# A hybrid linear-attention layer: the last set of 64x64 inverses taken up piece by piece inside the scan

## The chip, the cores and the metric

One core of a Trainium2 chip runs the whole layer in one launch. The metric is the device time of a run in microseconds (us); of several runs the median counts. The core's engines are TensorE (PE; its weight loads are listed as PEld), VectorE (DVE), ScalarE (ACT), GpSimd (POOL) and SyncE (SP), which here issues most DMA transfers. Each engine executes its instructions strictly in its own order; semaphores make them wait for one another.

## The reference

One layer: an adaLN-modulated RMSNorm, one input projection, and two token mixers side by side (a bidirectional chunked gated DeltaNet with 4 heads of 128, and windowed attention), then gates, projections and a residual. Sequence 2048 + 256 context tokens, width 1024. The part that the change concerns is the DeltaNet's chunk algebra (chunks of 64 tokens, two directions):

```python
a_mat = where(strict, einsum('nbhik,nbhjk->nbhij', kb, kc) * decay, 0)      # 64x64 per chunk and head
t_mat = triangular_solve(a_mat, eye, left_side=True, lower=True, unit_diagonal=True)
u = einsum('nbhij,nbhjv->nbhiv', t_mat, vc * bc)
w = einsum('nbhij,nbhjk->nbhik', t_mat, kb * exp(gc))
def step(s, xs):                              # sequential over the chunks
    v_new = u_n - einsum('bhck,bhkv->bhcv', w_n, s)
    s_new = s * exp(gl_n) + einsum('bhck,bhkv->bhkv', kd_n, v_new)
    o = einsum('bhck,bhkv->bhcv', qd_n, s) + einsum('bhij,bhjv->bhiv', qk_n, v_new)
```

Each `t_mat` is the inverse of a unit lower triangular 64x64 matrix. It depends on k, beta and the decays alone, not on the state, so all inverses can be had ahead of the scan.

## The kernel before, in words

The kernel runs in stages: norm and transposes, the state projection, q/k/v with their convolution, the products per chunk, then inverses, scan, attention, projections and output. The inverses are computed in three sets by forward substitution on DVE, 32 to 128 matrices side by side, one per partition. Two sets are made in `base`, beside matmuls of the gate projections. The last set is made by `base4`: it holds the 64-token blocks of the latent chunks 14 and 15 for the forward direction and 0 and 1 for the backward one (`LAST`), which the scan reaches only in its last two steps. It has 32 matrices, and each is handled as four groups of columns (column mod 4), so that it fills 128 partitions:

- two loads bring the raw blocks to `N` (L777, from `Nsp`), two more the betas;
- two DVE instructions scale `N` by columns and rows (L779, L780), each over all 64x64 of 32 partitions;
- three DMA copies take `N` to the other partitions (L784);
- 63 substitution rows of two DVE instructions each (L789 product into `btmp`, L791 sum into X, which is a slice of `btmp`);
- sixteen stores take X to DRAM (L796, `X4sp`).

The scan has 18 steps, each with both directions; step 0 and 1 are the context. A step of `chain` is, per direction: ksps = k·S on PE (L1085), x on DVE (L1087), vps on PE (L1091), v on DVE (L1094), sps on PE (L1103) and the state S on DVE (L1109); x begins as a load of v (L1077) with a multiplication on POOL (L1078). `merge` (L975 on) prepares the next step's 128x128 inverse from the 64x64 ones: it loads them (L995) or, for `LAST`, loads four parts into the single buffer `x4` (L990) and interleaves them on POOL (L991), then transposes (mtp: L1004, L1006), multiplies (myp, L1014 and L1016, scaled on DVE by L1018; mep, L1021 and L1023). `output` computes aps (L1126) and ops (L1137), with DVE's L1131, L1134 and L1138; partial outputs go to `osp` and come back when the other direction reaches the chunk.

Beside the scan run gate projections: `rps` matmuls (L524 to L526), 24 to a group, with their weight splits (L246 on DVE, L245 on POOL) and an `rt` step on DVE (L812). They do not depend on the scan and fill PE.

What sets the order: a scheduler takes instructions by priority with a model of the engines' timeline, and writes one fixed order for each engine. The scan is emitted at a higher priority than the gates around it. `base4` is emitted ahead of the scan, so its instructions are ahead of the scan's in priority; where they stand is what the scheduler makes of their readiness.

```python
    base4(*LAST)
    ...
        gates(list(range(4)), (1, 0))
        with tc.high_priority(tc.cur_priority):
            scan(scp, scl, cs)
        gates(list(range(4, BESIDE)), (1, 0))
```

The functions that the change touches, with their line numbers:

## Time and profile before

| | us |
|---|---|
| runs | 2027.2, 2026.38, 2021.74; median 2026.38 |
| profiled execution | 2024.6, span of its instructions 2022.9 |
| PE busy | 1943.7 (96%) |
| DVE busy | 1413.3 (70%) |
| ACT, POOL busy | 786.9 (39%), 656.8 (32%) |
| mean granted clock of TensorE | 0.986 of full |

The busy times are sums over the whole span; what an engine waits for is seen in the view of waits (for each line: what it waited for, total, times, longest) and in the timeline, where brackets hold the idle time ahead of an instruction and what ended it. The windows give each engine's busy time in a stretch and the granted clock there. The scan with its gates lies between 925 and 1375 us of the span.

### The profile page before, as it was taken

What the parts mean: (1) busy time and instruction counts of PE and PEld (TensorE: products, weight loads), DVE (VectorE), ACT (ScalarE), POOL (GpSimd) and SP (SyncE); (2) the same over time, 40 slices, a digit from 0 to 9 for tenths busy, and PEclk for the clock granted to TensorE, in tenths of its full rate; (3) what the DMA queues carried; (4) which work ended last, traced back from release to release, by engine and by line L of the source; (5) the groups of instructions that cost most, each with busy time, mean ns of one, the idle gap of its engine ahead of it and who ended that gap; (6) DMA issues with size and microseconds to landing.
All of it is one profiled execution on the core that took longest, in us unless ns stands there. A gap on an engine that the chain in (4) does not pass through costs nothing. (4 is left out here: it accounts for less than half of the span.)

```text
span 2022.9 us, 32038 instructions
## 1 busy us (share of the span) xinstructions
PE 1943.7 (96%) x11043; PEld 1630.9 (81%) x11043; DVE 1413.3 (70%) x2774; ACT 786.9 (39%) x1975; POOL 656.8 (32%) x751
## 2 busy tenths in 40 slices
PE   6999999989999899999999999999989999999999
PEld 3888888779898778787788888878777888878887
DVE  7979766667776999999699556635676878743322
ACT  6755545554343322111122223325665656531100
POOL 1742210224542211004222234323555443442221
PEclk8999999999999999999999999999999999999999
DMA  7552326755447633528877777664455555365542
GB/s 259 168 138 85 95 88 159 198 151 163 143 144 190 164 115 109 144 86 234 206 222 213 219 230 218 196 190 156 146 167 173 183 161 169 113 190 181 181 146 94
DMA packets 375511, 333.11 MB, mean 165 GB/s; under 512 B 83833, under 2 KB 299185, under 8 KB 374709
## 3 DMA queue, kind: packets, MB, share of 16 engines
q1 hardware_dynamic: 347924, 288.59, 49.4%
q10 hardware_dynamic: 27424, 42.48, 5.9%
q8 instruction: 87, 1.43, 0.3%
q14 instruction: 76, 0.61, 0.1%
HBM read 220.28 MB, written 109.13 MB: 163 GB/s over the span
## 5 line engine op out<-in xcount | busy, mean ns | idle before, releaser
L524 PE MATMUL rps<-hh,wh 128*128 128x512 f32 x768 | 308.4, 402 | 6.4 <-DVE rt L812 5.1
L526 PE MATMUL rps<-hh,wl 128*128 128x512 f32 x768 | 308.6, 402 | 0.0
L525 PE MATMUL rps<-hl,wh 128*128 128x512 f32 x768 | 308.5, 402 | 0.0
L524 PEld LDWEIGHTS rps<-hh,wh 128*128 128x128 f32 x768 | 145.4, 189 | 41.8 <-DVE rt L812 5.5
L563 DVE SCALAR_TENSOR_TENSOR cacc<-y,cw,cacc 128x512 f32<-128x512 f32 (+1 forms) x224 | 162.3, 746 | 22.7 <-ACT cacc L561 18.6
L524 PE MATMUL lps<-hh,wh 128*128 128x512 f32 (+1 forms) x448 | 171.5, 383 | 0.3 <-ACT y L634 0.3
L525 PEld LDWEIGHTS rps<-hl,wh 128*128 128x128 f32 x768 | 145.4, 189 | 32.4
L526 PE MATMUL lps<-hh,wl 128*128 128x512 f32 (+1 forms) x448 | 171.4, 382 | 0.0
L526 PEld LDWEIGHTS rps<-hh,wl 128*128 128x128 f32 x768 | 145.4, 189 | 32.0
L525 PE MATMUL lps<-hl,wh 128*128 128x512 f32 (+1 forms) x448 | 171.2, 382 | 0.0
L938 DVE TENSOR_TENSOR pl<-pt,ph 128x512 fp32r<-128x512 f32 x156 | 105.4, 685 | 43.7 <-ACT ph L936 42.9
L936 ACT CAST ph<-pt 128x512 fp32r<-128x512 f32 x156 | 90.4, 585 | 112.2 <-PE pt L934 77.8
L910 DVE CUSTOM_DVE_ANT_0 pr<-sc,band,sk 128x640 f32<-128x640 f32 (+1 forms) x128 | 106.5, 862 | 33.8 <-PE sc L906 18.1
L810 ACT ACTIVATE rt<-rps 128x512 f32<-128x512 f32 x96 | 57.3, 597 | 176.2 <-PE rps L526 162.6
L749 DVE TENSOR_TENSOR N<-N,btmp 128x62 f32<-128x62 f32 (+30 forms) x124 | 116.8, 942 | 3.0
L920 POOL TENSOR_SCALAR pr<-pr,sm 128x640 f32<-128x640 f32 (+1 forms) x128 | 99.7, 800 | 56.5 <-DVE sm L918 40.9
L747 DVE TENSOR_TENSOR btmp<-N 128x62 f32<-128x62 f32 (+30 forms) x124 | 114.8, 926 | 3.1
L912 ACT ACTIVATE pr<-pr,sm 128x640 f32<-128x640 f32 (+1 forms) x128 | 104.0, 815 | 19.6 <-DVE sm L910 19.6
L1216 PE MATMUL pps<-yh,wph 128*128 128x512 f32 x256 | 105.2, 415 | 5.8 <-ACT yh L1198 4.3
L246 DVE TENSOR_TENSOR wl<-wr,wh 128x512 fp32r<-128x512 f32 x120 | 92.6, 787 | 24.6 <-POOL wh L245 22.3
L245 POOL TENSOR_SCALAR wh<-wr 128x512 fp32r<-128x512 f32 x72 | 47.7, 678 | 180.1 <-PE lps L525 97.1
L1217 PE MATMUL pps<-yl,wph 128*128 128x512 f32 x256 | 101.5, 397 | 0.0
(301 smaller groups left out, 4944.9 us busy)
## 6 DMA issues: line engine op xcount, KB each, us to landing
wr<-in_w_in_dram SPq DMA_DIRECT2D x120, 256.0 KB
kw<-Ksp SPq DMA_DIRECT2D x28, 384.0 KB
x<-vsp SPq DMA_DIRECT2D x36, 256.0 KB
k<-ksp SPq DMA_DIRECT2D x34, 256.0 KB
kT<-kTsp SPq DMA_DIRECT2D x34, 256.0 KB
wm<-in_w_mod_dram SPq DMA_DIRECT2D x16, 512.0 KB
xt<-in_x_dram SPq DMA_DIRECT2D x16, 512.0 KB
dtl<-Dsp SPq DMA_DIRECT2D x32, 256.0 KB
```

Source lines behind the costliest of these rows:

```text
L524: T.matmul(ps, lhsT=wh[:, k], rhs=xh[:, k], start=k == 0, stop=False)
L525: T.matmul(ps, lhsT=wh[:, k], rhs=xl[:, k], start=False, stop=False)
L526: T.matmul(ps, lhsT=wl[:, k], rhs=xh[:, k], start=False, stop=k == kt - 1)
L563: V.scalar_tensor_tensor(a, y[:, t:t + n], cw[:, m, t:t + 1], a, op0=ALU.mult, op1=ALU.add)
L747: V.tensor_tensor(tv, A[:, m + 1:, m].unsqueeze(2).to_broadcast([h1 + n, r, m]), A[:, m, 0:m].unsqueeze(1).to_broadcast([h1 + n, r, m]), o ...
L749: V.tensor_tensor(A[:, m + 1:, 0:m], A[:, m + 1:, 0:m], tv, op=ALU.add)
L910: V.tensor_tensor_reduce(s_, ps[:, o:768], band[:, b0:b0 + W + 256], -0.125, sk[:, 1, hd:hd + 1], ALU.add, ALU.min, sm[:, h, 1:2])
L912: S.activation(s_, s_, AF.Exp, scale=-1.0, bias=sm[:, h, 1:2], accum_out=sm[:, h, 2:3])
L920: G.tensor_scalar(p[:, h, :W + 256], p[:, h, :W + 256], sm[:, h, 3:4], 1.0, op0=ALU.mult, op1=ALU.mult)
L938: V.tensor_tensor(pl, pt, f32(ph), op=ALU.subtract)
L1216: T.matmul(ps, lhsT=wh[:, k, ms], rhs=hs[k], start=k == 0, stop=False)
L1217: T.matmul(ps, lhsT=wh[:, k, ms], rhs=ls[k], start=False, stop=False)
```

## The change

`base4` becomes a generator that is taken up in pieces. The first piece (loads and the memsets on POOL) stays ahead of the scan. The second (scaling and the three copies) is taken at the end of scan step 2, then six substitution rows at the end of each of steps 3 to 12, the last three rows and the sixteen stores at step 13. Each piece is emitted back at the priority that holds outside the scan's block (`high_priority(-after)`), and not ahead of that step's last state update on the engine concerned (`issue_after`). The scaling is cut in four groups of 16 rows, each over its columns up to the diagonal's block: 16, 32, 48 and 64.

```diff
-        sh = [32, 64, 64]
-        V.tensor_tensor(N[0:32], N[0:32], nc_.unsqueeze(1).to_broadcast(sh), op=ALU.mult)
-        V.tensor_tensor(N[0:32], N[0:32], nb[0:32].unsqueeze(2).to_broadcast(sh), op=ALU.mult)
         G.memset(X, 0.0)
         for q in range(4):
-            if q:
-                dma(N[q * 32:q * 32 + 32], N[0:32])
             G.memset(X[q * 32:q * 32 + 32].rearrange("p r s -> p (r s)")[:, 16 * q:16 * q + 976:65], 1.0)
+        yield
+        for q in range(4):
+            r, w = slice(q * 16, q * 16 + 16), q * 16 + 16
+            V.tensor_tensor(N[0:32, r, 0:w], N[0:32, r, 0:w], nc_[:, 0:w].unsqueeze(1).to_broadcast([32, 16, w]), op=ALU.mult)
+            V.tensor_tensor(N[0:32, r, 0:w], N[0:32, r, 0:w], nb[0:32, r].unsqueeze(2).to_broadcast([32, 16, w]), op=ALU.mult)
+        for q in range(1, 4):
+            dma(N[q * 32:q * 32 + 32], N[0:32])
+        yield
         for m in range(63):
...
             V.tensor_tensor(X[:, m + 1:, 0:n], X[:, m + 1:, 0:n], tv, op=ALU.add)
+            if m % 6 == 5:
+                yield
...
                     dma(X4sp[d, ci, q], X[p0:p0 + 8])
+        yield
...
-    base4(*LAST)
+    last_base = base4(*LAST)
+    next(last_base)
...
+                last_S[0] = i
...
+            if 2 <= st < NC - 2:
+                with tc.high_priority(-after), tc.issue_after(last_S[0].ins):
+                    next(last_base, None)
...
-        with tc.high_priority(tc.cur_priority):
-            scan(scp, scl, cs)
+        first = tc.cur_priority
+        with tc.high_priority(first):
+            scan(scp, scl, cs, first)
```

In the changed kernel the lines of the scan are 6 to 9 further down: S is L1117, x L1095, rt L818, moff's scaling L1025, L1138 is L1147, the scaling L784 and L785, the copies L787, the substitution L792 and L794, the stores L801, the reads of `X4sp` L997.

The orders differ from here up to the end of the scan alone. First place, DVE around scan step 2. `N` is scaled, `my` and `moff` belong to the merge, `S` is the state, `oa` an output; the piece runs from the merge's L1012 (L1019) to the first output after the scaling. Before:

```order
L1012 TENSOR_TENSOR my_10504<-mtp,br 64x256
L779 TENSOR_TENSOR N<-N,btmp 32x4096
L246 TENSOR_TENSOR wl<-wr,wh 128x512
L812 SCALAR_TENSOR_TENSOR rt<-rt,rps 128x512
L246 TENSOR_TENSOR wl<-wr,wh 128x512
L1109 SCALAR_TENSOR_TENSOR S_10439<-S_10318,tot,sps 128x128 x4
L1109 SCALAR_TENSOR_TENSOR S_10477<-S_10351,tot,sps 128x128 x4
L1018 TENSOR_TENSOR moff_10486<-myp,br 64x256
L780 TENSOR_TENSOR N<-N,nb 32x4096
L1138 TENSOR_TENSOR oa_10542<-ops,oa_10542 128x512
```

Now:

```order
L1019 TENSOR_TENSOR my_10357<-mtp,br 64x256
L246 TENSOR_TENSOR wl<-wr,wh 128x512
L818 SCALAR_TENSOR_TENSOR rt<-rt,rps 128x512
L246 TENSOR_TENSOR wl<-wr,wh 128x512
L1117 SCALAR_TENSOR_TENSOR S_10292<-S_10171,tot,sps 128x128 x4
L1117 SCALAR_TENSOR_TENSOR S_10330<-S_10204,tot,sps 128x128 x4
L784 TENSOR_TENSOR N<-N,btmp 32x16x16
L784 TENSOR_TENSOR N<-N,btmp 32x16x32
L784 TENSOR_TENSOR N<-N,btmp 32x16x48
L784 TENSOR_TENSOR N<-N,btmp 32x1024
L1025 TENSOR_TENSOR moff_10339<-myp,br 64x256
L1147 TENSOR_TENSOR oa_10395<-ops,oa_10395 128x512
```

The scaling has moved from ahead of both updates of S to behind them. On PE at the same place, 31 gate matmuls stood between the last ops of step 1 and the first ksps of step 3, then mep and the second ksps; now 14 stand ahead of both ksps, 10 more before mep, and 15 after aps before the next vps. The first substitution row (L789) stood behind `my` of step 3 and ahead of S; L792 now stands behind both S of step 3 and ahead of moff's scaling.

Second place, SP at the copies of `N` (x, k, kT, qT are the scan's loads, mx and moff the merge's). Before:

```order
L1082 DMA kT_10739<-kTsp 128x4x128
L997 DMA moff_10814<-offsp_91 64x256
L995 DMA mx_10810<-Xsp_0_95 64x4x64
L1142 DMA osp_101<-oa_10542 128x512
L1082 DMA kT_10777<-kTsp 128x4x128
L995 DMA mx_10810<-Xsp_0_95 64x4x64
L784 DMA N<-N 32x4096 x3
L813 DMA zbsp_122<-rt 128x512
```

Now:

```order
L1090 DMA kT_10653<-kTsp 128x4x128
L787 DMA N<-N 32x4096
L1004 DMA moff_10690<-offsp_91 64x256
L1002 DMA mx_10686<-Xsp_0_95 64x4x64 x2
L1127 DMA qT_10755<-qTsp 128x4x128
L819 DMA zbsp_122<-rt 128x512
L787 DMA N<-N 32x4096 x2
L1085 DMA x_10788<-vsp 128x512
```

One copy has moved ahead of the merge's loads of step 4, the other two behind them and just ahead of that step's x.

Third place, SP at the stores of X and the reads into `x4`. Before, while the scan was at its eighth step:

```order
L796 DMA X4sp<-btmp 8x1024 x2
L1118 DMA qT_11699<-qTsp 128x4x128
L990 DMA x_12862<-X4sp 64x4x16 x2
L1075 DMA k_11756<-ksp 128x512
L1082 DMA kT_11723<-kTsp 128x4x128
L995 DMA mx_11794<-Xsp_1_96 64x4x64 x2
```

Now, at its fourteenth:

```order
L801 DMA X4sp<-btmp 8x1024 x2
L1127 DMA qT_12948<-qTsp 128x4x128
L997 DMA x_12868<-X4sp 64x4x16 x2
L1090 DMA kT_12801<-kTsp 128x4x128
L997 DMA x_12868<-X4sp 64x4x16 x2
L1004 DMA moff_12879<-offsp_91 64x256
```

The stores have moved by some six steps and stand now among the loads of the steps that need X; of the four rounds of eight reads all come after them, where before the first was issued with the stores and three late. On PE the last mtp (L1006, of step 17) stands 13 gate matmuls behind the mtp of the other direction, which follows vps of step 16.

## The prediction

> **What bounds the kernel now.** First the page's totals, for the engine that is the bound.

> ```profile
> span 2022.9 us, 32038 instructions
> PE 1943.7 (96%) x11043; PEld 1630.9 (81%) x11043; DVE 1413.3 (70%) x2774; ACT 786.9 (39%) x1975; POOL 656.8 (32%) x751
> ```

> TensorE (PE) is busy for 96% of the span, so the change can pay only where PE stands. All of it lies in the scan; hence the view of waits next, limited to 925 to 1375 us, first PE's rows, then the four of VectorE (DVE) that matter.

> ```profile
> PE ksps L1085 <- DVE S L1109: 5.4, 2, 4.7
> PE aps L1126 <- DVE oa L1138: 3.2, 1, 3.2
> PE ops L1137 <- DVE oa L1131: 2.0, 1, 2.0
> PE sps L1103 <- DVE v L1094: 1.8, 2, 1.3
> PE rps L524 <- ACT rt L810: 1.3, 3, 0.7
> PE fps L1055 <- DVE oa L1048: 0.5, 1, 0.5
> ...
> DVE N L779 <- DMA N<-Nsp: 10.7, 1, 10.7
> DVE oa L1131 <- DMA oa<-osp: 6.4, 1, 6.4
> DVE btmp L789 <- DMA N<-N: 5.7, 1, 5.7
> ```

> The reader is to see two single stalls of PE (4.7 and 3.2 us), both named on DVE, and two single stalls of DVE (10.7 and 5.7 us) at instructions of the last inverse set, both on a DMA. The DVE timeline shows that they belong together.

> ```profile
> 975.66 0.43 DVE L1012 TENSOR_TENSOR my<-mtp,br 64x256 f32<-64x256 f32 x1
> 986.81 4.41 DVE L779 TENSOR_TENSOR N<-N,btmp 32x4096 f32<-32x4096 f32 x1 [10.72 <-DMA N<-Nsp]
> ...
> 994.04 2.14 DVE L1109 SCALAR_TENSOR_TENSOR S<-S,tot,sps 128x128 f32<-128x128 f32 x8
> 996.11 0.41 DVE L1018 TENSOR_TENSOR moff<-myp,br 64x256 f32<-64x256 f32 x1
> 996.44 4.40 DVE L780 TENSOR_TENSOR N<-N,nb 32x4096 f32<-32x4096 f32 x1
> ...
> 1014.37 0.26 DVE L789 TENSOR_TENSOR btmp<-N,btmp 128x63 f32<-128x63 f32 x1 [5.71 <-DMA N<-N]
> ...
> 1017.02 0.69 DVE L1138 TENSOR_TENSOR oa<-ops,oa 128x512 f32<-128x512 f32 x1
> ```

> Stall A: the scaling L779 waits for its blocks until 986.81, runs 4.41 us, and the state update S (L1109) of scan step 2 stands behind it and starts at 994.04. Stall B: the first substitution row L789 waits for the copies of N until 1014.37, and the output's L1138 stands behind it. PE's side, and what it costs in clock:

> ```profile
> 980.07 1.95 PE L1103 MATMUL sps<-v,k 128*128 128x128 f32 x16
> 982.56 0.71 PE L1137 MATMUL ops<-v,qd 128*128 128x128 f32 x4
> 995.20 2.08 PE L1085 MATMUL ksps<-S,kT 128*128 128x128 f32 x8 [4.70 <-DVE S L1109]
> 1017.77 2.08 PE L1126 MATMUL aps<-S,qT 128*128 128x128 f32 x8 [3.25 <-DVE oa L1138]
> 1174.63 1.98 PE L1137 MATMUL ops<-v,qd 128*128 128x128 f32 x8 [1.99 <-DVE oa L1131]
> 1257.77 1.16 PE L1085 MATMUL ksps<-S,kT 128*128 128x128 f32 x8
> 995.00:1000.00 5.00, 4.80 (x33) 4.46 (x33) 5.00 (x7) 0.76 (x2) 0.53 (x1) 0.50 0.58 167
> 1000.00:1005.00 5.00, 5.00 (x27) 4.21 (x27) 5.00 (x12) 0.60 (x1) 1.20 (x2) 0.93 0.71 190
> 1015.00:1020.00 5.00, 2.23 (x9) 2.21 (x10) 4.73 (x18) 0.00 (x0) 0.83 (x1) 0.77 1.06 326
> 1020.00:1025.00 5.00, 5.00 (x37) 4.16 (x37) 4.90 (x14) 0.60 (x1) 1.98 (x3) 0.88 0.62 202
> 1025.00:1050.00 25.00, 25.00 (x199) 22.05 (x195) 24.08 (x63) 6.44 (x17) 6.28 (x9) 1.00 0.70 210
> ```

> The last rows are windows: span, busy time of PE, weight load, DVE, ACT, POOL, then granted clock, DMA share, GB/s. After A the clock is 0.50 for 5 us and 0.93 for 5 more: 5 × 0.50 + 5 × 0.07 = 2.85 us lost. After B, eight matmuls take 2.08 us for 1.16 at full clock, and the clock is 0.88 in the window after: 0.9 + 5 × 0.12 = 1.5 us. So A costs 4.70 + 2.85 = 7.55 and B 3.25 + 1.5 = 4.75, together 12.3 us. That is all this change can remove there: from 1025 on PE is full though DVE is 24.08 of 25 us busy.

> **The change, part by part.**

> *Scaling out of S's way.* In the new order S follows two weight splits (L246) and one rt directly behind L1012; the scaling's first half stands behind S, its second half behind moff and L1138. sps ends at 982.0 (row at 980.07), so S runs 982.0 to 984.2. PE now has 14 gate matmuls instead of 31 ahead of ksps. In the old program 31 of them fill 983.3 to 990.5 (982.56 + 0.71, and 995.20 − 4.70), 0.235 us each; so 14 end at 986.6, after S. Stall A goes: −7.55 us, and with it what it held back.

> *Four parts instead of one.* The earlier sets (L737) have the same four forms on 64 partitions:

> ```profile
> L737 DVE TENSOR_TENSOR N<-N,nb x8: 418/810/1211, 645.0 to 666.0; 64x256 f32<-64x256 f32 x2, 64x512 f32<-64x512 f32 x2, 64x768 f32<-64x768 f32 x2, 64x1024 f32<-64x1024 f32 x2
> ```

> Two each of 0.42, 1.21 and two middle ones whose mean is 0.81: 0.42 + 1.62 + 1.21 = 3.25 us a scaling, 6.5 for both, against 4.41 + 4.40 = 8.8. DVE saves 2.3 us; none lies on PE's path once S stands ahead. Counted at nothing.

> *What is late next at A.* N's blocks still land at 986.81, so DVE waits 2.6 us behind S, scales to 990.1, runs moff 0.4 and L1138 0.7, scales to 994.4, then x (L1087, 2.1) to 996.5. PE after ksps (986.6 to 988.7) has 10 gates to 991.0, mep (needs moff, done 990.5), aps, 15 gates to about 995.5; vps wants x's first half at 995.5. PE waits 0 to 1 us; I give back 0.3.

> *Copies of N and the first rows.* SyncE (SP) issues the three copies in order with the scan's loads, and they wait for the second scaling.

> ```profile
> 979.24 1.15 SPq L777 DMA_DIRECT2D N<-Nsp  x2
> 1003.00 3.44 SPq L784 DMA_DIRECT2D N<-N  x3
> 1019.16 2.17 POOL L1078 TENSOR_TENSOR x<-x,rin 128x512 f32<-128x512 f32 x2 [11.46 <-DMA x<-vsp]
> ```

> Before, issue at 1003.00 and landing at 1014.37: 11.4 us. Now the first is issued at about 994.4, two more only after moff, two X loads, qT and a store (five issues of some 0.6 us, as the first row's 1.15 for two), and the loads of step 4's x behind them. Landing is 994.4 + 3 + 11.4 = 1008.8 at worst by that row, some 1006 if the shorter queue helps. The first row of the substitution now stands right behind S of step 3. A step takes about 21 us:

> ```profile
> 1235.21 1.11 DVE L1109 SCALAR_TENSOR_TENSOR S<-S,tot,sps 128x128 f32<-128x128 f32 x4
> 1292.07 0.61 PE L1091 MATMUL vps<-x,mw 128*128 128x128 f32 x4
> ```

> The upper row is S of step 13: (1235.2 − 994.0) / 11 = 21.9, less B and the stall at 1173 (7.6 in all) 21.2. So S of step 3 starts near 1003 and ends near 1005. DVE may then stand 1 to 4 us, with moff of step 3 behind it; PE holds aps, 7 gates, ksps and 3 gates (0.5 + 1.6 + 1.1 + 0.7 = 3.9 us) before mep needs moff. Step 4's x is a second way to the same wait. PE's share is between 0 and the 3.25 us of stall B; I take 1.4 and, by the row at 1174.63 (1.99 idle, then 1.98 for 1.16), 0.6 of clock: 2.0 us given back; the bounds are 0 and 4.75.

> [...]

> *Substitution spread.* Twelve DVE instructions a step in steps 3 to 12 instead of 52 us in a block:

> ```profile
> L791 DVE TENSOR_TENSOR btmp<-btmp 128x252 f32<-128x252 f32 (+52 forms) x63 | 26.5, 421 | 1.2
> L789 DVE TENSOR_TENSOR btmp<-N,btmp 128x252 f32<-128x252 f32 (+52 forms) x63 | 25.7, 409 | 7.0 <-DMA N<-N 5.7
> ```

> 52.2 / 10.5 = 5 us a step of about 21. The same instructions, so no time of their own, and in the window from 1025 to 1050 PE was full beside the block. Nothing, then, but later steps whose DVE was free of it now carry 5 us. The stall at 1173 (the reload of the output's partial sum, 6.4 us of DVE, then PE's 1.99 and about 0.8 of clock) is a store's and a load's trip, and its neighbours on DVE keep their order: unchanged; bounds −2.8 and +2.

> *The tail.* The sixteen spills of X now come in step 13, not before 1120.7 (the first read, below), and the reads into the one x4 buffer, two rounds of eight for each of the last two steps, follow within some 60 us.

> ```profile
> L990 SPq DMA_DIRECT2D x<-X4sp x32: 573/608/647, 1120.7 to 1277.1; - x32
> L991 POOL COPY mx<-x x8: 620/638/702, 1242.0 to 1281.4; 64x256 f32<-64x256 f32 x8
> 1281.39 0.64 POOL L991 COPY mx<-x 64x256 f32<-64x256 f32 x1 [5.84 <-DMA x<-X4sp]
> ```

> A round is 8 × 0.61 of issue, up to 5.84 of waiting and two copies of 0.64: 12 us; four make 48. X ends a few us behind S of step 13, at about 1238 before and, 9 us earlier, 1229 now: the last copy comes near 1277. Its reader is the last transpose (mtp, L1006) of step 17, in the new order 13 gates behind vps of step 16 (the row at 1292.07, now about 1283): 1283 + 0.6 + mtp + 3.1, some 1288. So it is hidden by 11 us if the queue keeps step, but the spills and rounds stand in SP between kT, qT, k and x of steps 14 to 16. Below: nothing. Above: one more wait of 5.84 on PE's path. I take 2.0, a third.

> Sum: −12.3 + 0.3 + 2.0 + 2.0 = −8.0 us. On the profiled execution (2024.6 us, span 2022.9) that is 2016.6; on the median of the runs, 1.8 above it, 2018.4. I say 2017.

> **The rivals.** Apart from a real change stands 0.3%, 6 us, about what a measurement of this kernel can tell from none.

> *No change: the stalls only move.* The DMA share of the 5 us around B is 1.06, so the wait for copies and for x may stay whole (4.75 given back), and the tail may take its 5.84 besides. −12.3 + 0.3 + 4.75 + 5.84 = −1.4: 2023. For it: DVE waited on a DMA, not on its own work, at both stalls, and the data comes no sooner at A. Against it: at A, the larger, S no longer stands behind the wait.

> *Slower: the four rounds through the one x4 buffer come late.* Each round must wait for the copies of the one before, each copy stands in POOL's order behind other work, and SP issues a round in pieces between loads. At 19 us a round instead of 12 the last copy comes at 1229 + 76 = 1305, 17 us after its reader's place, and PE, whose order is fixed, stands: 2016.6 − 2.0 + 17 = 2032. It costs from 14.8 us a round on ((1288 − 1229) / 4) and decides from 18.7 on, where 16 us are lost (2030.7). For it: in the trace the copies of the four rounds run from 1242.0 to 1281.4, 13 us a round, though the first was loaded long ahead. Against it: those rounds were called for no sooner.

> *A larger gain.* If N's copies land before S of step 3 ends, the tail hides and the stall at 1173 goes as well: −12.3 − 2.8 + 0.3 = −14.8, 2010. For it: DVE and PE get earlier, not the store queue, so the reload could also worsen.

> **How the numbers follow.** My forecast 0.49 (2013 to 2020), larger gain 0.11, no change 0.30, slower 0.10. The range for 8 in 10 runs from the larger gain's 2009 up to 2026, the no-change case with 3 us more for the median's place above the profiled run and for the tail: it leaves out the slower case and a little at either end. Faster by over 0.3% means under 2020.3: 0.49 + 0.11 = 0.60; within 0.30; slower 0.10.

> **What the new profile would show.** PE's row ksps <- S of 4.7 us is gone, and S of step 2 starts near 982 to 984; clock 1.00 in that window. The scaling's first part still waits on N<-Nsp, some 2 to 3 us, with no PE row to match. The first substitution row waits on N<-N, less than 5.7 us; a PE row on mep or vps of 1 to 2 us there is my give-back. In the tail the copies L991 come in a row from about 1235 to 1277; PE rows of L1006 waiting for L991 tell whether that costs. I am wrong if PE's idle time over the scan, about 14 us now, does not fall by at least 4, or if PE waits at the last L1006 or on kT, k or x behind the spills.

## The result, and the profile after

The changed kernel takes 2009.32 us (median of 4 runs, 2004.02 to 2014.64) where the kernel before takes 2026.18 (4 runs): ratio 0.9918, 95% interval 0.9894 to 0.9942. Beside later kernels it was timed again: 2010.89 (6 runs) against 2023.91, ratio 0.9934 (0.9912 to 0.9955). It is faster by 13 to 17 us, where 9 were forecast; 2009.3 lies just inside the range.

The page's totals of the changed kernel, then PE's waits from 925 to 1375 us (line, what it waited for, total, times, longest), then the DVE waits that answer to those shown before:

```profile
span 2009.1 us, 32070 instructions
PE 1936.4 (96%) x11043; PEld 1625.3 (81%) x11043; DVE 1407.5 (70%) x2780; ACT 786.1 (39%) x1975; POOL 654.0 (33%) x751
PE ksps L1093 <- DVE S L1117: 2.9, 1, 2.9
PE mep L1028 <- DVE moff L1025: 1.8, 1, 1.8
PE sps L1111 <- DVE v L1102: 1.3, 1, 1.3
PE rps L524 <- ACT rt L816: 1.0, 2, 0.7
PE ops L1146 <- DVE oa L1140: 1.1, 1, 1.1
...
DVE N L784 <- DMA N<-Nsp: 3.5, 1, 3.5
DVE oa L1140 <- DMA oa<-osp: 3.3, 1, 3.3
DVE btmp L792 <- issue: 0.8, 1, 0.8
```

The rows of 4.7 and 3.2 us are gone, and two smaller ones are new, at mep (1.8) and on S, at another place (2.9). The reload of a partial output (ops) is 1.1 where it was 2.0. DVE still waits for N's blocks, 3.5 us, and no longer for the copies of N. The timeline of DVE and the one PE row at the first place:

```profile
982.11 2.15 DVE L1117 SCALAR_TENSOR_TENSOR S<-S,tot,sps 128x128 f32<-128x128 f32 x8
987.77 4.71 DVE L784 TENSOR_TENSOR N<-N,btmp 32x256 f32<-32x256 f32 x4 [3.50 <-DMA N<-Nsp]
992.40 0.41 DVE L1025 TENSOR_TENSOR moff<-myp,br 64x256 f32<-64x256 f32 x1
...
993.34 3.01 DVE L785 TENSOR_TENSOR N<-N,nb 32x256 f32<-32x256 f32 x4
...
1008.30 1.12 DVE L1117 SCALAR_TENSOR_TENSOR S<-S,tot,sps 128x128 f32<-128x128 f32 x4 [0.22 <-PE sps L1111]
1010.22 0.27 DVE L792 TENSOR_TENSOR btmp<-N,btmp 128x63 f32<-128x63 f32 x1 [0.80 <-issue]
992.86 0.27 PE L1028 MATMUL mep<-moff,mx 64*64 64x64 f32 x1 [1.77 <-DVE moff L1025]
988.37 3.03 POOL L1086 TENSOR_TENSOR x<-x,rin 128x512 f32<-128x512 f32 x2 [8.04 <-DMA x<-vsp]
975.00:1000.00 25.00, 23.23 (x162) 19.66 (x162) 17.84 (x35) 4.98 (x14) 6.37 (x7) 1.00 0.98 245
1000.00:1025.00 25.00, 25.00 (x183) 21.69 (x182) 17.37 (x43) 8.01 (x23) 6.11 (x9) 1.00 0.97 275
```

S of step 2 is at 982.11 instead of 994.04. The wait for the blocks stands behind it, and what it holds up is moff, for which PE waits 1.77 us. The first row of the substitution runs at 1010.22 and waits for no DMA. The last two rows are the windows of 25 us over both old stalls (PE busy, weight load, DVE, ACT, POOL, granted clock, DMA share, GB/s): PE has 23.23 and 25.00 us of work where it had 20.30 and 21.75, at clock 1.00 where it had 0.88 and 0.92.

**An account of the scan.** Waits do not hold the whole difference, so PE's time was divided in three, from the first ksps to the start of the attention's 257th score matmul, the 129th by `kw` (the end that the expectations call the 128th): 3853 matmuls, as many of each kind in every kernel. The parts are the idle time (all gaps between matmuls; the timeline's brackets show those over 0.15 us); half of the time worked in windows where the granted clock is 0.5; and the rest, which is what the matmuls take from start to start. "Changes of kind" counts, in PE's order, how often a matmul is followed by one of another name (gate, ksps, mep and so on).

| kernel | span | idle | lost to half clock | rest | changes of kind |
|---|---|---|---|---|---|
| before | 616.5 | 25.1 | 9.5 | 581.9 | 586 |
| changed | 597.6 | 17.6 | 3.4 | 576.6 | 551 |
| changed, second profile | 604.8 | 21.7 | 6.8 | 576.3 | 551 |

The difference of 18.9 us is 7.5 of idle time, 6.1 of clock and 5.3 of rest. In the second profile idle time and clock have given 7.5 back, and the rest is the same within 0.3.

### The profile page after: what moved, and what is told of

Read it like the earlier page. It is cut to its first block, busy times and chain, and to the rows that moved or that the text cites. A ratio compares the mean times of both kernels' runs of the same rounds, so it can differ in the third digit from the quotient of the medians.

```text
span 2009.1 us, 32070 instructions
## 1 busy us (share of the span) xinstructions
PE 1936.4 (96%) x11043; PEld 1625.3 (81%) x11043; DVE 1407.5 (70%) x2780; ACT 786.1 (39%) x1975; POOL 654.0 (33%) x751
## 5 line engine op out<-in xcount | busy, mean ns | idle before, releaser
L524 PE MATMUL rps<-hh,wh 128*128 128x512 f32 x768 | 308.4, 402 | 5.4 <-DVE rt L818 4.2
L524 PEld LDWEIGHTS rps<-hh,wh 128*128 128x128 f32 x768 | 145.0, 189 | 40.1 <-DVE rt L818 4.8
L524 PE MATMUL lps<-hh,wh 128*128 128x512 f32 (+1 forms) x448 | 171.4, 383 | 0.2 <-ACT y L634 0.2
L246 DVE TENSOR_TENSOR wl<-wr,wh 128x512 fp32r<-128x512 f32 x120 | 91.6, 776 | 23.9 <-POOL wh L245 21.3
```

What stands on the lines that cost most here:

```text
L524: T.matmul(ps, lhsT=wh[:, k], rhs=xh[:, k], start=k == 0, stop=False)
```

## The experiments

Three theories came out of this. Theory 1: the gain is the place of the scaling and of the first row, behind S instead of ahead of it. Theory 2: besides, the new order of PE is worth 5 us, because it changes less often from one kind of matmul to another. Theory 3: whether a stall is followed by half clock is chance. Rivals: the shorter scaling, or the spreading over ten steps, is what pays. Kernels that ran together share the runs of the kernel before, whose median was 2026, 2028, 2021 and 2024 us in the four sets; so ratios are compared, and accounts of the traces.

**1. The cut alone.** Only the scaling of the kernel before is replaced:

```diff
-        V.tensor_tensor(N[0:32], N[0:32], nc_.unsqueeze(1).to_broadcast(sh), op=ALU.mult)
-        V.tensor_tensor(N[0:32], N[0:32], nb[0:32].unsqueeze(2).to_broadcast(sh), op=ALU.mult)
+        for q in range(4):
...
```

> The scaling in four parts, everything else as before. Theory 1: DVE still waits for N's blocks ahead of S until about 987, so S comes only the 1.2 us earlier by which the first scaling is shorter (4.4 to 3.2), and PE's stalls of 4.7 and 3.2 us and the half-clock windows stay in the main: 2022 to 2026 us, ratio 0.998 to 1.000. Rival, the cut is what pays: below 2016.

2028.49 us, ratio 1.0006 (0.9991 to 1.0021), just above the range. The cut alone brings nothing. Its waits, PE then DVE, and the rows of stall B:

```profile
PE ksps L1086 <- DVE S L1110: 6.3, 1, 6.3
PE aps L1127 <- DVE oa L1139: 5.2, 2, 4.2
PE ops L1138 <- DVE oa L1135: 3.1, 1, 3.1
DVE N L780 <- DMA N<-Nsp: 11.7, 1, 11.7
DVE btmp L790 <- DMA N<-N: 6.5, 1, 6.5
...
1007.93 0.26 DVE L790 TENSOR_TENSOR btmp<-N,btmp 128x63 f32<-128x63 f32 x1 [6.48 <-DMA N<-N]
1008.40 0.68 DVE L1135 TENSOR_TENSOR oa<-aps,npre 128x512 f32<-128x512 f32 x1
1009.13 1.16 PE L1138 MATMUL ops<-v,qd 128*128 128x128 f32 x8 [3.05 <-DVE oa L1135]
```

Stall A is there (6.3 us on S), and so is stall B: the first substitution row waits 6.5 us for the copies, an output stands behind it, and PE waits 3.1 us, now at ops. The row at aps is not B: its 4.2 us stand at 1158 us, behind a gate's weight split that waits 6.5 us for POOL. That stall is new, for here too the scheduler wrote other orders (569 changes of kind), so the time is no clean price of the cut. The mechanism of theory 1 holds, from its other side: with the scaling ahead of S and the first row ahead of an output, both stalls stay.

**2. The pieces without the cut.**

```diff
-        for q in range(4):
...
+        V.tensor_tensor(N[0:32], N[0:32], nc_.unsqueeze(1).to_broadcast(sh), op=ALU.mult)
+        V.tensor_tensor(N[0:32], N[0:32], nb[0:32].unsqueeze(2).to_broadcast(sh), op=ALU.mult)
```

> The pieces stay, but the scaling is two whole instructions again (4.4 us each) instead of four parts. Theory 1, the gain comes from where the scaling and the first row stand (behind S, not ahead of it): PE's wait for moff at step 2, 1.77 us with four parts, grows by the 1.2 us that the first scaling is longer, to about 3, and may now bring a half-clock window (1.7 us); otherwise nothing: 2011 to 2014 us, ratio to before about 0.993. Rival, the shorter scaling is a good part of the gain: over 2018 us.

2020.77 us, ratio 0.9973 (0.9959 to 0.9987). By the time alone the rival wins: over 2018, two thirds of the gain are gone. The trace tells otherwise. Stalls A and B are both gone without the cut. The wait for moff is not 3 us but 0.2, and the largest stall is a new one, 2.9 us at aps, at 1033 us (PE's rows, then DVE's):

```profile
PE aps L1134 <- DVE oa L1146: 3.6, 2, 2.9
PE mep L1027 <- DVE moff L1024: 0.2, 1, 0.2
...
1030.13 1.08 DVE L246 TENSOR_TENSOR wl<-wr,wh 128x512 fp32r<-128x512 f32 x1 [5.75 <-POOL wh L245]
1031.24 0.69 DVE L817 SCALAR_TENSOR_TENSOR rt<-rt,rps 128x512 f32<-128x512 f32 x1
1031.85 0.81 DVE L246 TENSOR_TENSOR wl<-wr,wh 128x512 fp32r<-128x512 f32 x1
1032.58 0.68 DVE L1146 TENSOR_TENSOR oa<-ops,oa 128x512 f32<-128x512 f32 x1
```

A gate's weight split waits 5.75 us for POOL, and the output and S stand behind it: the same pattern as A, made by another instruction. The account: idle 19.9, half clock 4.7, rest 583.5, with 584 changes of kind. 6.9 us of what it lost on the changed kernel are rest: the scheduler, given other durations, wrote other orders. Theory 1 had no term for that; it is why the next runs count it.

**3. No spreading.** `if m % 6 == 5: yield` is left out, so that all rows and stores come at the end of step 3.

> Scaling at step 2 as changed, but all 63 substitution rows and the sixteen stores taken at the end of step 3 in one piece, not six rows a step. Theory 1: A and B are gone all the same, DVE is nearly full from step 3 to 8 as it was before, without a stall of PE, and the stores come some 100 us earlier, so that the 2.9 us stall of the tail goes too: 2006 to 2011 us. Rival, it is the spreading over ten steps that pays (DVE never in S's way): stalls on S, v or x of several us in steps 3 to 8, 2015 us or more.

2015.60 us, ratio 0.9944 (0.9921 to 0.9966): by the time, which is 2015 or more, the rival has it. The trace tells otherwise. No stall of PE of 1.5 us or more stands in steps 3 to 8; idle 18.9 and half clock 3.2 are about the changed kernel's 17.6 and 3.4. So the spreading is not needed to keep DVE out of S's way. The rest is 582.4 with 584 changes, 5.8 us more than the changed kernel, and that is the loss. The stores 100 us earlier did not remove the tail's stall (the row at ksps, at 1275 us):

```profile
PE ksps L1091 <- DVE S L1115: 2.9, 1, 2.9
PE mep L1026 <- DVE moff L1023: 2.5, 1, 2.5
```

**4. One step later.** The condition is `3 <= st` and `m % 8 == 7`.

> The scaling taken at step 3 instead of 2, eight rows a step from step 4, so that the stores come at step 11. Theory 1: N's blocks have landed long before (987 against about 1010), so PE's 1.77 us for moff go or shrink to the 3 us of DVE work ahead of it; the stores two steps earlier take away some of the queue behind which qd comes late in the tail (2.9 us): 2005 to 2009 us, 1 to 4 us under the changed kernel. Rival, these two waits cost nothing on the whole (the gates fill elsewhere): the same 2009 as the changed kernel within 1 us.

2011.48 us, ratio 0.9921 (0.9903 to 0.9939): the changed kernel's ratio, 2.5 us above the range. Idle time is 3.7 us lower (14.0), as expected, and no PE row names moff; the rest is 6.3 higher (582.9, 600 changes), which was not.

**5. to 8. Orders of PE chosen by their count.** Since the count is known before a run, four kernels were picked for it. Nine or twelve rows a step (`m % 9 == 8`, `m % 12 == 11`), the scaling at step 4 with ten rows (`4 <= st`, `m % 10 == 9`), and the pieces put behind the last output instead of behind S:

```diff
-            V.tensor_tensor(oa, ops_, oa, op=ALU.subtract)
+            last_S[0] = V.tensor_tensor(oa, ops_, oa, op=ALU.subtract)
```

> Nine substitution rows a step instead of six; the stores come at step 10 instead of 13. On PE the order has 556 changes from one kind of matmul to another between the first ksps and the 128th score matmul of the attention, the changed kernel 551, the kernel before 586. Theory 2 (PE's time between its stalls hangs on the number of these changes, 5.3 us for 35 in the two traces, 0.15 us each): 0.8 us more than the changed kernel for the order, and up to 2.9 less where the reads of X no longer hold back the tail: 2007 to 2011. Rival (the order of PE costs nothing, the stalls are all): 2006 to 2007 if the tail's stall goes, 2009 if not. The two are near here; the run is the low end of a series with the next but one.

> Twelve rows a step, stores at step 8: 564 changes of kind on PE. Theory 2: 13 x 0.15 = 2.0 us more than the changed kernel for the order, less what the tail's stall of 2.9 us gives back: 2008 to 2011. Rival (stalls alone): the tail's 2.9 us go, 2006; DVE gets twice the rows a step, so S may wait in steps 3 to 8, 2010.

> The scaling at step 4 instead of 2, ten rows a step, stores at step 11: neither of the two places of the change is near a late DMA (N's blocks land at 987, step 4 is past 1025), so PE should stand less than in the changed kernel; but its order has 615 changes of kind, 64 more. Theory 2: the time between the stalls is 9 to 10 us longer than in the changed kernel (64 x 0.15), the whole 2014 to 2018 us. Rival (stalls alone): no more than the changed kernel, 2005 to 2009.

> Each piece of the set is put behind the step's last output on DVE (L1147) instead of behind its last state update, six rows a step. moff of step 2 then stands ahead of the scaling, so PE's 1.77 us at mep go; the copies of N leave a few us later and the first row may wait, with little behind it. 570 changes of kind on PE, 19 more. Theory 2: -1.8 + 19 x 0.15 = +1.1 us against the changed kernel, 2009 to 2012. Rival (stalls alone): 1.8 us less, 2007; or more if the late copies make a new stall.

| kernel | us | ratio to before | idle | half clock | rest | forecast of the rest |
|---|---|---|---|---|---|---|
| nine rows | 2015.44 | 0.9965 (0.9951 to 0.9980) | 21.1 | 1.7 | 577.9 | 577.4 |
| twelve rows | 2012.43 | 0.9951 (0.9935 to 0.9968) | 18.7 | 0.0 | 580.9 | 578.6 |
| step 4, ten rows | 2015.93 | 0.9976 (0.9964 to 0.9987) | 19.9 | 5.0 | 587.6 | 586.2 |
| behind the output | 2019.26 | 0.9994 (0.9982 to 1.0006) | 23.8 | 8.5 | 580.5 | 579.5 |

The rest follows the count within 2.3 us, and the kernel with 615 changes has the longest rest of all, 11 us above the changed kernel, though neither old stall is in it. Of the times only that of step 4 lies in its range; the others are 4.4, 1.4 and 7.3 us above, though the kernel before was 5 us quicker in this set: new stalls, of which theory 2 says nothing. Behind the output the stall at mep is gone, as expected, and worse ones have come, 3.5 us at aps and 3.2 at ops, where theory 2 had given 1.1 us in all. Ahead of them on DVE:

```profile
1035.37 1.69 DVE L246 TENSOR_TENSOR wl<-wr,wh 128x512 fp32r<-128x512 f32 x2 [6.38 <-POOL wh L245]
1036.98 0.67 DVE L818 SCALAR_TENSOR_TENSOR rt<-rt,rps 128x512 f32<-128x512 f32 x1
1037.58 0.68 DVE L1147 TENSOR_TENSOR oa<-ops,oa 128x512 f32<-128x512 f32 x1
...
1266.83 0.69 DVE L1055 TENSOR_TENSOR oa<-oa,fss 128x512 f32<-128x512 f32 x1 [8.26 <-POOL fss L1054]
```

The pattern once more, with the split of a gate's weights and with the finished output's scale.

**9. The changed kernel again.**

> The changed kernel once more, beside the next three on one chip: ratio to before 0.992 again, and as in its first profile 551 changes of kind on PE with about 576.6 us of PE time between the stalls (from the first ksps to the 128th score matmul, half-clock time taken out). How far stalls and half-clock windows differ from the first profile tells how much of those is chance: theory 3, that a stall of 1.8 to 3 us brings a half-clock window or not by chance, expects differences there of up to 3.4 us, and no more than 0.5 us in the time between.

Ratio 0.9934, and the rest differs by 0.3 us, as expected. Idle time is 4.1 and half clock 3.4 us higher: more than "up to 3.4" in all, since the stalls themselves differ. Its waits, and a window of 5 us at mep:

```profile
PE ksps L1093 <- DVE S L1117: 4.5, 2, 4.3
PE ops L1146 <- DVE oa L1140: 2.1, 1, 2.1
PE mep L1028 <- DVE moff L1025: 1.8, 1, 1.8
990.00:995.00 5.00, 5.00 (x32) 4.53 (x33) 5.00 (x12) 0.76 (x2) 1.33 (x2) 0.66 1.04 283
```

The same wait of 1.8 us at mep that left the clock at 1.00 in the first profile (window 975 to 1000) is followed by 0.66 here.

**10. to 12. The pieces at the scan's priority.** `with tc.issue_after(last_S[0].ins):` alone, without the lower priority; then with twelve rows a step; then with `3 <= st` and eight rows.

> The pieces keep the scan's own priority instead of the one outside it; all else as changed. DVE's order at step 2 is the same, so A stays gone and the 1.8 us at mep stay. PE has 542 changes of kind, 9 fewer than the changed kernel. Theory 2 (0.16 us a change): 1.5 us less between the stalls, 575.1; the whole 2006 to 2010 where the changed kernel has 2009. Rival (rows of the set now ahead of the gates' splits and rt on DVE, gates wait): PE rows on rt or wl, 2 us or more above the changed kernel.

> As the last, with twelve rows a step, so that the stores come at step 8 and the reads of X are spread: 556 changes of kind. Theory 2: 577.4 us between the stalls; the tail's stall of 2.9 us (qd behind the reads in SP's order) is gone: 1 to 3 us under the changed kernel. Rival (the tail's stall has another cause): a stall on S near 1265 is there again, equal to the changed kernel or slower.

> Scaling at step 3, eight rows a step, at the scan's priority: the counterpart of the run that began at step 3 (600 changes of kind, 582.9 us between the stalls), now with 572. Theory 2: 28 x 0.16 = 4.5 us less between the stalls, 578.4, no stall at mep of step 2, so 2 to 4 us below the changed kernel if no new stall comes. Rival (the count is no cause): 582 to 583 us between the stalls as in that run.

| kernel | us | ratio to before | idle | half clock | rest | forecast of the rest |
|---|---|---|---|---|---|---|
| scan's priority | 2017.94 | 0.9979 (0.9966 to 0.9992) | 20.2 | 11.5 | 574.8 | 575.1 |
| ..., twelve rows | 2020.77 | 0.9983 (0.9966 to 1.0000) | 25.2 | 3.9 | 580.4 | 577.4 |
| ..., from step 3 | 2016.49 | 0.9977 (0.9961 to 0.9994) | 18.0 | 3.3 | 582.9 | 578.4 |

The fewest changes give the shortest rest, 574.8; but the other two miss, by 3.0 and 4.5 us, the last exactly where its rival put it. Over the fourteen traces (thirteen kernels) the rest rises by 0.152 us a change, and the points lie 1.2 us about that line (correlation 0.92). The count is a fair measure, not the whole cause; what else there is stays open. No run changed the order of PE alone.

The traces tell more of what the count stands for. Most matmuls of the merge, 592 of the 656 in this stretch, work on 64 rows, all others on 128. PE's order changes between these shapes 130 times before, 106 times in the changed kernel and 151 times in the one with 615 changes of kind. Take as the pace of a kind the median interval, from start to start, to a matmul of the same kind. Against that pace the intervals at a change of shape and directly beside one lose 23.4 us before, 18.8 in the changed kernel (18.6 in its second profile) and 28.2 in the one with 615 changes; all other intervals lose 20.9, 20.2 (20.1) and 21.8. So by this measure some 4.6 of the 5.3 us, and 9.4 of the 11, lie where the shape changes.

All three are slower than the changed kernel beside which they ran (2010.89), the first by idle time and half clock (20.2 and 11.5 us). Its wait for the split weights (rps on wh) is 2.3 us, 0.6 in the changed kernel's second profile, as the rival said. No other kernel beat the changed one.

In the second of the three the tail's stall was expected to be gone with the early stores. It is there, 4.2 us at 1271, and its rows show the cause better than the changed kernel's did. First the changed kernel, then this one; POOL's row of fss, what stands ahead of it, and DVE's L1055 that needs it, with S behind:

```profile
1262.29 0.63 POOL L1131 TENSOR_SCALAR_AFFINE_SELECT qd<-qd 128x512 f32<-128x512 f32 x1 [5.11 <-DMA qd<-QDsp]
1262.89 0.20 POOL L1054 TENSOR_TENSOR fss<-fss,alpha 128x4 f32<-128x4 f32 x1
1263.12 1.50 DVE L1055 TENSOR_TENSOR oa<-oa,fss 128x512 f32<-128x512 f32 x1 [5.06 <-POOL fss L1054]
1264.55 1.11 DVE L1117 SCALAR_TENSOR_TENSOR S<-S,tot,sps 128x128 f32<-128x128 f32 x4
1265.71 1.16 PE L1093 MATMUL ksps<-S,kT 128*128 128x128 f32 x8 [2.89 <-DVE S L1117]
```

```profile
1272.33 0.61 POOL L998 COPY mx<-x 64x256 f32<-64x256 f32 x1 [4.55 <-DMA x<-X4sp]
1273.02 0.20 POOL L1054 TENSOR_TENSOR fss<-fss,alpha 128x4 f32<-128x4 f32 x1
1273.25 1.09 DVE L1055 TENSOR_TENSOR oa<-oa,fss 128x512 f32<-128x512 f32 x1 [5.25 <-POOL fss L1054]
1274.27 1.11 DVE L1117 SCALAR_TENSOR_TENSOR S<-S,tot,sps 128x128 f32<-128x128 f32 x4
```

In both, a 0.2 us instruction on POOL stands behind one that waits for a load, once qd and once a part of X; DVE waits 5 us for it, and S stands behind DVE's wait. It is stall A in small, with POOL as a further link. Early stores do not remove this chain: it cost PE 2.9 us in the third experiment, and with twelve rows a step at the lower priority DVE still waits 2.9 us for fss, of which 0.2 reach PE. A kernel that moves L1054 ahead of such loads was not tried.

## Why the prediction was right, step by step

The sign, the place and the first term were right; the size was right by half. The recorded sum is −8.0, which is 2018.4 on the median of the runs; the forecast of 2017 stands 1.4 below its own sum.

- **Stall A and stall B** (−7.55 and −4.75 forecast): both are gone, also without the cut, and the cut alone, which leaves the scaling ahead of S, keeps both. The clock was sized a little low: the half-clock windows at the two places and at 1174 cost 6.1 us (half of the time worked in them), where the sum has 2.85 + 1.5 and names 0.8.
- **What is late next at A** (0.3 forecast): mis-sized. PE waits 1.77 us, and 1.8 with half clock behind it in the second profile. The blocks landed at 987.77, 1.0 us later than the walk had it, and the first half of the scaling took 4.71 us where the four forms had given 3.25; the other half took 3.01. The walk added durations from another place and did not see that POOL multiplies x there (988.37, 3.03 us).
- **Copies of N** (2.0 given back): nothing. The first row came at 1010.22, later than the 1005 of the walk, since S of step 3 was at 1007 to 1009.4, and the data was there.
- **The reload at 1173** (unchanged): it fell to 1.1 us without half clock in one profile and is 2.1 us with it in the other. The bounds held it.
- **The tail** (2.0, bounds 0 and 5.84): 2.9 and 4.3 us, within the bounds; but the place was wrong. It was to be the last mtp (now L1013) waiting for the copies of X; no PE row of either profile does. (One did in the second experiment, by 1.7 us.) The stall is the chain over POOL's L1054.
- **What the sum had no term for**: the order of PE. The prediction took the same matmuls to need the same time in any order. 5.3 us of the gain are PE's time apart from idle time and clock (5.6 in the second profile), some 4.6 of them at changes of shape, and the counts that go with it were to be had beforehand from the orders: 586 and 551 changes of kind. This is the step that makes the forecast too small; with it the sum would have been about −13. That the order is the cause rests on this account and on the forecasts made from the count, not on a run that changed the order alone.

By the sign that it named for being wrong, PE's idle time over the scan (about 14 us in the rows of the waits) had to fall by at least 4. It fell to 8.3 in the first profile and only to 12.2 in the second: what the waits alone give is not steady from one execution to the next.

Of the rivals, "a larger gain" (−14.8) came nearest, by other means than it named: N's copies were in time, but the tail did not hide. "The rounds come late" did not come true.

## What to carry to other kernels

Look for a wait on a DMA that stands in front of a serial chain on an engine whose order is fixed (at the first place DVE started S at 982.11, N at 987.77 and moff at 992.40, as printed above): the price is everything behind it. Moving the waiting instruction behind the chain's next link paid here though its data came 1.0 us later (987.77 against 986.81): PE, which had stood 4.7 us for S, stood 1.8 for moff. Where a scheduler rewrites an engine's order, compare the two orders as a whole: count how often the bound engine changes its kind of work, the shape of its matmuls above all: here the time went up with that count even where nothing waited, by 0.152 us a change. And take more than one profile: two of the same program had 21.0 and 28.6 us of idle time and lost clock in the scan and the attention's start.

## What the runs showed of the hardware

**Changes of shape.** The timeline of the kernel before, where two 64x64 matmuls stand between gate matmuls (start, duration):

```profile
1109.99 0.39 PE L525 MATMUL rps<-hl,wh 128*128 128x512 f32 x1
1110.22 0.40 PE L526 MATMUL rps<-hh,wl 128*128 128x512 f32 x1
1110.55 0.33 PE L1014 MATMUL myp<-mw,moff 64*64 64x64 f32 x2
1110.81 0.50 PE L524 MATMUL rps<-hh,wh 128*128 128x512 f32 x1
1111.14 0.40 PE L525 MATMUL rps<-hl,wh 128*128 128x512 f32 x1
```

Gate matmuls start 0.23 us apart. The one before the small pair is followed after 0.33, the pair takes 0.26, and the first gate after it is followed after 0.33 again: 0.46 us more than without the pair, where two such matmuls inside a group of sixteen take less than 0.1 (0.06 from 1126.80 to 1126.86 in the changed kernel). That puts a price on a change of shape here; what PE does in that time, the rows do not show.

**Half clock.** All stalls of PE of 1.5 us or more in the scan, over the fourteen traces, and whether a window of half clock (3.4 us, or two of them) began with them or behind them:

| stall | with half clock | without |
|---|---|---|
| 1.51 to 1.77 us | 0 | 6 |
| 1.80 to 2.94 us | 14 | 7 |
| 3.05 to 6.28 us | 9 | 0 |

**DVE beside POOL.** The same four scaling forms took 4.71 us while POOL multiplied x (988.37, 3.03 us for two, where two took 2.17 in the kernel before at 1019.16) and 3.01 us a little later. The two forms that began ahead of POOL's x took 0.41 and 0.67 us both times; the two beside it took 1.78 and 2.05, and later 0.94 and 1.21. In the kernel before, DVE's scaling took 4.41 us beside POOL's x (from 987.28) and 4.40 without it (from 996.44); there the two multiplications of x took 6.29. Why now DVE and now POOL is the slower, no run shows.
